# Seven-product SwiGLUs: the w2 product behind two block products, two weight sums by accumulating transfers, token operands formed later

## The chip, the cores and the metric

One core of one Trainium2 chip runs the whole program in one launch. The metric is the device time of that core in microseconds. The kernel before takes 2764.49 us (median of 3 runs, 2763.46 to 2766.02).

## The reference

A two-layer backbone over 512 latent tokens and 256 context tokens of width 1024. Each layer is a half-step SwiGLU, a token mixing, and another half-step SwiGLU; each is preceded by an RMS norm with shift and scale and followed by a gate, and these come from a modulation of a conditioning vector. The change is in the SwiGLUs:

```python
def swiglu(x, w1, w3, w2):
    return (jax.nn.silu(x @ w1) * (x @ w3)) @ w2

def macaron_half(h, m, i, g, w1, w3, w2):
    y = swiglu(modulate(rms_norm(h, g), m[:, 3 * i], m[:, 3 * i + 1]), w1, w3, w2)
    return h + 0.5 * m[:, 3 * i + 2, None, :] * y
```

D_MODEL is 1024 and D_FF 2816. All is float32. The modulation of a layer is `silu(c) @ w_ada[l] + b_ada[l]`, nine vectors of 1024 for the latent and nine for the context tokens.

## The kernel before

Tokens lie in columns (768: first 256 context, then 512 latent), channels on the partitions. To keep float32 accuracy, each operand of a matmul is split into a high and a low part (`hi`, `lo`, both fp32r): ScalarE makes `hi` by a cast, VectorE `lo` by a subtraction (`split_psum`, L403 and L404; with a factor L406 and L407). A product is then three matmuls, hi*hi, hi*lo and lo*hi (`mm3`, L396 to L398).

There are four SwiGLUs. The first runs in a plain form (`ffn`). The other three run in `ffn7`: the second of layer 0 (here A, from about 1003 us), the first of layer 1 (B, from about 1552 us), and the second of layer 1 (C, from about 2420 us, latent tokens alone). `ffn7` goes over the 22 hidden tiles of 128 channels in 11 pairs. The first pair (`first_pair`) is computed plainly. The other ten (`pair(j, ...)`) multiply the 2x2 blocks of weights (2 hidden tiles by 2 halves of the 1024 inputs, w1 and w3 side by side, 128x1024 elements each, blocks r11, r12, r21, r22) by the 2x2 blocks of tokens (2 halves of the inputs by 2 halves of the columns) with seven block products instead of eight, in the manner of Winograd. They are called by their token operand: B11, B21, E, t3, t1, t4, B22. Each is 24 matmuls (2 of w1/w3, 4 of 128 inputs, 3 of hi/lo), of 384 columns in A and B and of 256 in C. B11, B21 and B22 are plain blocks of the normed tokens; E, t4, t3 and t1 are combinations of the kept float32 tokens (`t`, tiles `nf`), formed once for each SwiGLU by `combine` (L835 to L838, sixteen subtractions and additions in all, and the splits) and `combine_rest`. The weights of E, t3, t1 and B22 are sums of blocks, formed in every pair by four VectorE additions (L973, L974, L975, L977). The seven products go to two PSUM areas, Y and X; `snapshot` (ScalarE, L888) copies an area out where a later product is added to it, and `gated` and L993/L994 form silu(w1 part) * (w3 part) into `silu` tiles. `parts` (L869, L870) splits these into `ghi` and `glo`, the token operand of the w2 product.

The w2 product of a pair (`down`, 8 output tiles for the latent and 8 for the context columns; 96 matmuls, in C 48) goes through four PSUM banks B; VectorE adds each result to `h` (L905) and so frees its bank. It is handed to the next pair as `middle()`, and stands there behind the first block product, B11. After each w2 product, `modulate(j)` takes groups of the modulation of layer 1 from a queue: each loads four `ada` tiles (L491) and has VectorE multiply and sum them (`mod_tile`, L483, tile `junk`), with a priority that is 3000 instructions later. `mods` says how many groups each pair takes: one in A's pairs 1 to 8, two in B's.

Weights come through five `raw` buffers (`block`, L798; for w2 `unit`, L388), all by transfers issued by SP, and their split parts through four `w` buffers. Working tiles come from 44 slots that are handed out first in, first out (`m3`, `free`). The order of the instructions on each engine is laid out when the program is built, by a scheduler that takes of the instructions that its model of time has ready the one with the earliest place in the program; each engine then runs its own in that order, and waits where an operand or a buffer isn't there.

Of the kernel before, what the change touches and what calls it, by code (L numbers as in the profile page):

```python
# [12 lines left out]
ALU = mybir.AluOpType  # L13
# [5 lines left out]
T = CTX + SEQ  # L19
# [293 lines left out]
class Builder:  # L313
# [480 lines left out]
    def block(self, src):  # L794

        r = self.mp.tile([128, 1024], F32, tag="raw", name=self.name("raw"), bufs=self.raws)
        if src is not None:
            self.nc.sync.dma_start(r, src)  # L798
        return r

    def split_block(self, r, scale=None):
# [4 lines left out]
    def ffn7(self, l, i, n, t, gate, nxt, streams=(X_COLS, C_COLS), split=None, late=None, mods=()):  # L806
# [14 lines left out]
        halves = X_HALVES if x_only else ((0, T // 2), (T // 2, T))  # L821
        wd = halves[0][1] - halves[0][0]
        n1, n2 = (slice(*c) for c in halves)
        off = {X_COLS: 512, C_COLS: 256}
        np_ = NF // 2
# [2 lines left out]

        tt, box, owned = {}, {}, []

        def combine(k):

            u, v = t[k], t[k + 4]
            tensor = nc.vector.tensor_tensor
            tensor(out=u[:, n1], in0=u[:, n1], in1=u[:, n2], op=ALU.subtract)  # L835
            tensor(out=u[:, n2], in0=v[:, n2], in1=u[:, n2], op=ALU.subtract)
            tensor(out=v[:, n2], in0=u[:, n1], in1=v[:, n2], op=ALU.add)
            tensor(out=v[:, n1], in0=v[:, n2], in1=v[:, n1], op=ALU.subtract)  # L838
            c = slice(halves[0][0], halves[1][1])
            hi, lo = self.hl(T, "c")  # L840
            self.split_psum(hi[:, c], lo[:, c], v[:, c])
            tt[k, "t4"], tt[k, "E"] = ([p[:, q] for p in (hi, lo)] for q in (n1, n2))
            owned.append((hi, lo))
            if k % 2 == 0:
                box["t3"] = self.hl(2 * wd, "c")
                owned.append(box["t3"])
            tt[k, "t3"] = [p[:, k % 2 * wd:k % 2 * wd + wd] for p in box["t3"]]
            self.split_psum(*tt[k, "t3"], u[:, n2])
            self.free(t.pop(k + 4))

        def combine_rest():

            for k in range(4):
                tt[k, "t1"] = [p[:, n2] for p in n[k]]
                self.split_psum(*tt[k, "t1"], t[k][:, n1])
                self.free(t.pop(k))

        def operand(name, k):
            if name in ("B11", "B21", "B22"):
                return [p[:, n1 if name[2] == "1" else n2] for p in n[k + 4 * (name[1] == "2")]]  # L860
            return tt[k, name]


        def gtiles(j):
            for f in (2 * j, 2 * j + 1):
                g[f] = self.hl(T, "g")

        def parts(f, s, cols):
            nc.scalar.copy(g[f][0][:, cols], s[:, cols])  # L869
            nc.vector.tensor_sub(g[f][1][:, cols], s[:, cols], g[f][0][:, cols].bitcast(F32))  # L870

        def product(bank, w, name, start):

            for x in range(2):
                for k in range(4):
                    self.mm3(bank[:, x * 512:x * 512 + wd], [w[:, p, x * 512 + k * 128:x * 512 + k * 128 + 128] for p in range(2)],
                             operand(name, k), start and k == 0, k == 3, not start)
# [7 lines left out]
        def snapshot(bank, base):  # L885
            y = self.m3(2 * wd, base=base)
            v = y.rearrange("p (x c) -> p x c", x=2)
            nc.scalar.copy(v, both(bank))  # L888
            return y, v

        def gated(s, cols, bank, y, sign):

            zv = y[1]
            nc.vector.tensor_tensor(out=zv, in0=both(bank), in1=y[1], op=ALU.add)
            self.last_silu = nc.scalar.activation(s[:, cols], zv[:, 0], AF.Silu, scale=sign)
            nc.vector.scalar_tensor_tensor(out=s[:, cols], in0=zv[:, 1], scalar=sign, in1=s[:, cols], op0=ALU.mult, op1=ALU.mult)
# [59 lines left out]
        def pair(j, middle):  # L956
            fs = (2 * j, 2 * j + 1)
            src = mp13[j]
            add = nc.vector.tensor_add
            Y, X = (self.ps("S", (j + x) % 2) for x in range(2))  # L960
            r11 = self.block(src[0, 0])
            product(Y, self.split_block(r11), "B11", True)
            middle()
            y0 = snapshot(Y, "y")
            gtiles(j)
            s = [self.m3(base="silu") for _ in range(2)]
            r12 = self.block(src[0, 1])
            product(X, self.split_block(r12), "B21", True)
            r21, r22, s1 = self.block(src[1, 0]), self.block(src[1, 1]), self.block(None)
            gated(s[0], n1, X, y0, 1.0)  # L970
            self.free(y0[0])
            parts(fs[0], s[0], n1)
            add(s1, r21, r22)  # L973
            add(r21, r11, r21)  # L974
            add(r11, s1, r11)  # L975
            product(Y, self.split_block(r11, -1.0), "E", False)
            add(r12, r11, r12)  # L977
            y1 = snapshot(Y, "y")
            product(X, self.split_block(r21), "t3", True)
            w0 = snapshot(X, "y")  # L980
            if j == 1:
                combine_rest()
            product(Y, self.split_block(s1), "t1", False)
            gated(s[1], n2, Y, w0, -1.0)
            self.free(w0[0])
            product(X, self.split_block(r22), "t4", False)
            if j == np_ - 1:
                self.free(owned)
            gated(s[1], n1, X, y1, -1.0)
            self.free(y1[0])  # L990
            parts(fs[1], s[1], slice(halves[0][0], halves[1][1]))
            product(Y, self.split_block(r12), "B22", False)
            self.last_silu = nc.scalar.activation(s[0][:, n2], Y[:, 0:wd], AF.Silu)  # L993
            nc.vector.tensor_mul(s[0][:, n2], s[0][:, n2], Y[:, 512:512 + wd])  # L994
            parts(fs[0], s[0], n2)
            self.free(s)

        self.table(AF.Silu, self.norm_sqrt)
        first_pair()
        for k in range(4):  # L1000
            combine(k)

        def middle(j):
            def go():
                ws, fs = second(j), (2 * j, 2 * j + 1)
                for d in range(8):
                    for cols in streams:
                        down(fs, ws, d, cols)
                self.free([g.pop(f) for f in fs])
                modulate(j)  # L1010
            return go
# [737 lines left out]
    def build(self, stop=None):  # L1749
        nc = self.nc  # L1750
        self.setup()
        n = self.new_n()
        begin = Start(self, n)
        for g in range(5, 24):
            self.mod_queue.append(lambda g=g: self.mod_group(0, g, 16))
        for l in range(DEPTH):
            last = l == DEPTH - 1
            ns = 1 if last else 2
            nxt = Next(self, l, 3, SM_GMIX, 2, n)
            if l:  # L1760
                tabs = []
                self.ffn7(l, 0, n, t, self.gate(l, 2, 2, 0.5), nxt, late=lambda: tabs.extend(self.rope_tables(l)), mods=(2,) * 8)
            else:
                self.ffn(l, 0, n, self.gate(l, 2, 2, 0.5), nxt, begin=begin, mods=2)
            assert not self.mod_queue
            if l == 0:
                tabs = self.rope_tables(l)
                self.setup_mixing()
            if stop == (l, 0):
                break  # L1770

            nxt = Next(self, l, 6, SM_GF2, ns, keep=True)
            self.mixing(l, n, tabs, self.gate(l, 5, ns, 1.0), last, nxt)
            n, before = nxt.n, nxt
            if stop == (l, 1):
                break

            if not last:
                self.load_small(l + 1)
                self.silu_c(wide=True)  # L1780
                for g in range(24):
                    self.mod_queue.append(lambda g=g: self.mod_group(1, g))
                nxt = Next(self, l + 1, 0, SM_GF1, 2, n, keep=True)
                self.ffn7(l, 1, n, before.t, self.gate(l, 8, 2, 0.5), nxt, mods=(1,) * 8)
                t = nxt.t
            else:
                self.ffn7(l, 1, n, before.t, self.gate(l, 8, 1, 0.5), Done(self), streams=(X_COLS,), split=X_HALVES)
            if stop == (l, 2):
                break
        if stop is not None:  # L1790
            for k in range(8):
                nc.sync.dma_start(self.a["out"][k], self.h[k])
# [122 lines left out]
```

## Time and profile before

| | |
|---|---|
| median of 3 runs | 2764.49 us (2763.46 to 2766.02) |
| profiled execution's own time | 2769.52 us |
| its span, first to last instruction | 2767.7 us |
| mean granted TensorE clock | 0.984 |
| TensorE matmul busy | 2658.0 us, 96% |
| VectorE busy | 2046.8 us, 74% |
| ScalarE busy | 1087.9 us, 39% |
| GpSimd busy | 278.8 us, 10% |
| read from HBM | 244.90 MB, 89 GB/s over the span |

An engine is busy while one of its instructions runs; overlapping matmuls count once. The granted clock is the share of full TensorE speed (2.4 GHz) that was granted; in this trace a stretch is at 1.0 or at 0.5 (1.2 GHz), and a mean between them says how much of it was at the lower level. "A <- B" in a list of waits says that A's next instruction was ended in its waiting by B. Because the engines run in order, a wait delays all that stands behind it on its engine.

### The profile page before, as it was taken

The page shows a single profiled execution, that of the slowest core. Times are in us where ns is not written, and L with a number is a line of the kernel's source. Part 1 is how long each engine was busy: PE and PEld are TensorE (multiplying, and loading weights), DVE is VectorE, ACT ScalarE, POOL GpSimd, SP SyncE. Part 2 cuts the span into 40 slices and gives each one's busy share as a digit, 9 for nine tenths or more (in the row PEclk, how much of TensorE's full clock was granted, in tenths as well). Part 3 has the DMA queues.
Part 4 walks back from the last instruction along what each step waited for, and adds up shares of the span by engine and source line. Part 5 has one row for each costly group of instructions (what it writes and reads, how often), then busy time and mean ns, then how long its engine had stood idle before and what let it go on. Part 6 is the DMA issues. An engine that isn't in the chain of part 4 may idle for free.

```text
span 2767.7 us, 40029 instructions
## 1 busy us (share of the span) xinstructions
PE 2658.0 (96%) x15788; PEld 2357.8 (85%) x15788; DVE 2046.8 (74%) x3551; ACT 1087.9 (39%) x1895; POOL 278.8 (10%) x370
## 2 busy tenths in 40 slices
PE   7999999999989998999999989999999989999999
PEld 5788888888867788999899879999998877888998
DVE  8986776655775559778676799887756675587886
ACT  4311211124665653233232632323335665544443
POOL 5100000001352210000000100000001352100000
PEclk8899999999989999999999999999999999999999
DMA  7542433211200013233222244443222210123322
GB/s 246 162 136 94 158 117 113 83 54 56 75 22 24 12 46 111 90 102 99 81 75 69 67 125 128 141 144 121 84 76 67 69 32 24 39 80 106 98 93 91
DMA packets 78673, 249.60 MB, mean 90 GB/s; under 512 B 8978, under 2 KB 10642, under 8 KB 78484
## 3 DMA queue, kind: packets, MB, share of 16 engines
q1 hardware_dynamic: 78484, 247.03, 27.6%
q8 instruction: 124, 2.03, 0.3%
q14 instruction: 65, 0.53, 0.1%
HBM read 244.90 MB, written 2.10 MB: 89 GB/s over the span
## 4 chain that ended last, share of the span: by engine, by line
PE 78%; DVE 14%; ACT 3%; issue 3%; DMA 2%; POOL 0%; SPq 0%; DVEq 0%; ACTq 0%; POOLq 0%
PE S L396 14%; PE S L398 13%; PE S L397 13%; PE B L397 10%; PE B L398 10%; PE B L396 10%; PE B L1424 3%; DVE w L404 2%; DVE junk L483 2%; PE B L1575 2%; DVE h L905 1%; DMA raw<-in_w13s 1%; DMA ada<-in_w_ada 1%; ACT w L403 1%; PE B L1543 1%
## 5 line engine op out<-in xcount | busy, mean ns | idle before, releaser
L403 ACT CAST w<-raw 128x1024 fp32r<-128x1024 f32 (+1 forms) x369 | 381.3, 1044 | 723.3 <-issue 330.0
L397 PE MATMUL S<-nlo,w 128*128 128x256 f32 (+2 forms) x1808 | 598.0, 331 | 9.4 <-DVE nlo L605 6.2
L396 PE MATMUL S<-nhi,w 128*128 128x256 f32 (+2 forms) x1808 | 590.0, 332 | 12.7 <-DVE silu L994 4.3
L398 PE MATMUL S<-nhi,w 128*128 128x256 f32 (+2 forms) x1808 | 596.4, 331 | 2.7 <-DVE w L404 2.5
L404 DVE TENSOR_TENSOR w<-raw,w 128x1024 fp32r<-128x1024 f32 (+1 forms) x369 | 449.2, 1229 | 95.3 <-ACT w L403 94.2
L397 PE MATMUL B<-glo,w 128*128 128x512 f32 (+1 forms) x1232 | 425.4, 346 | 5.6 <-DVE glo L870 5.6
L398 PE MATMUL B<-ghi,w 128*128 128x512 f32 (+1 forms) x1232 | 423.0, 346 | 3.1 <-DVE w L404 3.1
L396 PE MATMUL B<-ghi,w 128*128 128x512 f32 (+1 forms) x1232 | 416.2, 348 | 6.4 <-DVE h L905 2.7
L905 DVE SCALAR_TENSOR_TENSOR h<-B,g,h 128x512 f32<-128x512 f32 (+1 forms) x440 | 273.3, 642 | 145.5 <-PE B L398 144.7
L397 PEld LDWEIGHTS S<-nlo,w 128*128 128x128 f32 x1808 | 343.6, 190 | 33.8 <-DVE nlo L605 10.5
L396 PEld LDWEIGHTS S<-nhi,w 128*128 128x128 f32 x1808 | 341.4, 190 | 35.7 <-DVE silu L994 4.3
L398 PEld LDWEIGHTS S<-nhi,w 128*128 128x128 f32 x1808 | 344.2, 190 | 25.8 <-DVE w L404 6.9
L397 PEld LDWEIGHTS B<-glo,w 128*128 128x128 f32 x1232 | 232.0, 188 | 35.5 <-DVE glo L870 6.5
L396 PEld LDWEIGHTS B<-ghi,w 128*128 128x128 f32 x1232 | 229.8, 188 | 37.8 <-DVE h L905 5.1
L483 DVE CUSTOM_DVE_ANT_0 junk<-ada,bc,mpart 128x768 f32<-128x768 f32 x238 | 245.6, 1032 | 20.3 <-DMA ada<-in_w_ada 16.9
L398 PEld LDWEIGHTS B<-ghi,w 128*128 128x128 f32 x1232 | 231.7, 188 | 33.8 <-DVE w L404 3.8
L396 PE MATMUL S<-chi,w 128*128 128x384 f32 (+1 forms) x720 | 232.1, 323 | 13.5 <-ACT y L888 10.7
L398 PE MATMUL S<-chi,w 128*128 128x384 f32 (+1 forms) x720 | 229.1, 321 | 2.7 <-DVE w L404 2.1
L397 PE MATMUL S<-clo,w 128*128 128x384 f32 (+1 forms) x720 | 230.5, 321 | 0.0
L691 DVE SCALAR_TENSOR_TENSOR h<-B,g,h 128x256 f32<-128x256 f32 (+1 forms) x176 | 103.8, 615 | 101.6 <-PE B L398 101.6
L532 POOL TENSOR_TENSOR sq<-sq,sq 128x512 f32<-128x512 f32 (+1 forms) x38 | 42.2, 1112 | 1159.3 <-ACT sq L528 1158.1
L888 ACT COPY y<-S 128x768 f32<-128x768 f32 (+1 forms) x90 | 65.5, 728 | 237.7 <-PE S L398 130.9
(267 smaller groups left out, 4413.6 us busy)
## 6 DMA issues: line engine op xcount, KB each, us to landing
raw<-in_w SPq DMA_DIRECT2D x132, 512.0 KB, 3.6
raw<-in_w13s SPq DMA_DIRECT2D x132, 512.0 KB, 3.8
ada<-in_w_ada SPq DMA_DIRECT2D x171, 384.0 KB, 4.0
raw<-in_w_out SPq DMA_DIRECT2D x16, 512.0 KB, 4.3
ada<-in_ada SPq DMA_DIRECT2D x16, 384.0 KB, 6.4
raw<-in_w_in_t SPq DMA_DIRECT2D x10, 512.0 KB, 3.5
raw<-in_dftx SPq DMA_DIRECT2D x8, 512.0 KB, 3.5
ada<-in_ada SPq DMA_DIRECT2D x8, 256.0 KB, 5.2
```

What stands on the lines that cost most here:

```text
L396: mm(out, lhs[0], rhs[0], start=start, stop=False, skip_group_check=more)
L397: mm(out, lhs[0], rhs[1], start=False, stop=False, skip_group_check=more)
L398: mm(out, lhs[1], rhs[0], start=False, stop=stop, skip_group_check=more)
L403: nc.scalar.copy(hi, src)
L404: nc.vector.tensor_sub(lo, src, hi.bitcast(F32))
L483: nc.vector.tensor_tensor_reduce(out=self.junk[:, 0:w.shape[1]], in0=w, in1=v, scale=1.0, scalar=init, op0=ALU.mult, op1=ALU.add, accum_ou ...
L532: (nc.vector if part else nc.gpsimd).tensor_add(st[key], st[key], t)
L691: nc.vector.scalar_tensor_tensor(out=self.h[d][:, c0:c1], in0=ps[:, 0:c1 - c0], scalar=gate()[:, d, s:s + 1], in1=self.h[d][:, c0:c1], op0 ...
L888: nc.scalar.copy(v, both(bank))
L905: nc.vector.scalar_tensor_tensor(out=self.h[d][:, c0:c1], in0=ps[:, 0:c1 - c0], scalar=gate()[:, d, s:s + 1], in1=self.h[d][:, c0:c1], op0 ...
L1424: mm(outs[y], lhs[y], rhs[y], start=start, stop=stop)
L1575: nc.tensor.transpose(pt[:, x * 256 + i * 128:x * 256 + i * 128 + 128], Ps[i, y][:, tok(kp * 2 + x)], self.ident)
```

## The change

- In `pair`, the weights of B11 and B21 are loaded first; both products stand ahead of `middle()`, so a pair's w2 product stands behind two block products of the next pair. New `g` tiles are taken after it.
- Two of the four sums leave VectorE. `block_sum` loads the first block with SP and adds the second by a transfer that GpSimd issues with `accum_op=ALU.add`: s1 = r21 + r22 and s3 = r11 + r21 (the former r21). r22 is loaded by itself; r11 and r21 are read twice. A pair has seven loads of w1/w3 blocks instead of four.
- `combine` is called by operand within pair 1: "E" behind the w2 product, "t4" and "t3" (with t1) behind E; before, all but t1 was formed between `first_pair` and pair 1. The sum for B22 stands behind t1.
- The groups of modulation move from pairs 1 to 8 to pairs 3 to 10 (`mods`), in A and B.

```diff
+    def block_sum(self, *srcs):
+        r = self.block(srcs[0])
+        for src in srcs[1:]:
+            self.nc.gpsimd.dma_start(out=r, in_=src, accum_op=ALU.add)
         return r
...
-        def combine(k):
...
+        def combine(name):
             for k in range(4):
+                u, v = t[k], t[k + 4]
+                if name == "E":
+                    tensor(out=u[:, n1], in0=u[:, n1], in1=u[:, n2], op=ALU.subtract)
+                    tensor(out=u[:, n2], in0=v[:, n2], in1=u[:, n2], op=ALU.subtract)
+                    tensor(out=v[:, n2], in0=u[:, n1], in1=v[:, n2], op=ALU.add)
+                    tensor(out=v[:, n1], in0=v[:, n2], in1=v[:, n1], op=ALU.subtract)
+                    box[k] = self.hl(T, "c")
+                    owned.append(box[k])
+                    parts_of("E", k, [p[:, n2] for p in box[k]], v[:, n2])
+                elif name == "t4":
+                    parts_of("t4", k, [p[:, n1] for p in box[k]], v[:, n1])
+                    self.free(v)
+                else:
+                    parts_of("t1", k, [p[:, n2] for p in n[k]], u[:, n1])
...
+                    parts_of("t3", k, [p[:, k % 2 * wd:k % 2 * wd + wd] for p in box["t3"]], u[:, n2])
+                    self.free(u)
...
-            r11 = self.block(src[0, 0])
+            first = combine if j == 1 else lambda name: None
+            r11, r12 = self.block(src[0, 0]), self.block(src[0, 1])
             product(Y, self.split_block(r11), "B11", True)
-            middle()
             y0 = snapshot(Y, "y")
-            gtiles(j)
+            product(X, self.split_block(r12), "B21", True)
             s = [self.m3(base="silu") for _ in range(2)]
-            r12 = self.block(src[0, 1])
-            product(X, self.split_block(r12), "B21", True)
-            r21, r22, s1 = self.block(src[1, 0]), self.block(src[1, 1]), self.block(None)
             gated(s[0], n1, X, y0, 1.0)
             self.free(y0[0])
+            middle()
+            gtiles(j)
             parts(fs[0], s[0], n1)
-            add(s1, r21, r22)
-            add(r21, r11, r21)
+            s1, s3, r22 = self.block_sum(src[1, 0], src[1, 1]), self.block_sum(src[0, 0], src[1, 0]), self.block(src[1, 1])
+            first("E")
             add(r11, s1, r11)
             product(Y, self.split_block(r11, -1.0), "E", False)
-            add(r12, r11, r12)
             y1 = snapshot(Y, "y")
-            product(X, self.split_block(r21), "t3", True)
+            first("t4")
+            first("t3")
+            product(X, self.split_block(s3), "t3", True)
             w0 = snapshot(X, "y")
-            if j == 1:
-                combine_rest()
             product(Y, self.split_block(s1), "t1", False)
             gated(s[1], n2, Y, w0, -1.0)
             self.free(w0[0])
+            add(r12, r11, r12)
             product(X, self.split_block(r22), "t4", False)
...
-        for k in range(4):
-            combine(k)
...
-                self.ffn7(l, 0, n, t, self.gate(l, 2, 2, 0.5), nxt, late=lambda: tabs.extend(self.rope_tables(l)), mods=(2,) * 8)
+                self.ffn7(l, 0, n, t, self.gate(l, 2, 2, 0.5), nxt, late=lambda: tabs.extend(self.rope_tables(l)), mods=(0,) * 2 + (2,) * 8)
...
-                self.ffn7(l, 1, n, before.t, self.gate(l, 8, 2, 0.5), nxt, mods=(1,) * 8)
+                self.ffn7(l, 1, n, before.t, self.gate(l, 8, 2, 0.5), nxt, mods=(0,) * 2 + (1,) * 8)
```

## Rows read from the trace of the kernel before

**Rows 1.** Page, part 1: busy us, share of the span, instructions.
```profile
PE 2658.0 (96%) x15788; PEld 2357.8 (85%) x15788; DVE 2046.8 (74%) x3551; ACT 1087.9 (39%) x1895; POOL 278.8 (10%) x370
```
**Rows 2.** Stretches: length, each engine's busy us, granted clock, DMA share, GB/s.
```profile
1035.00:1104.00 69.00, 62.04 (x350) 57.13 (x348) 67.56 (x124) 28.59 (x42) 0.00 (x0) 0.98 0.36 111
1104.00:1401.00 297.00, 284.54 (x1569) 269.01 (x1569) 231.31 (x382) 88.63 (x113) 0.00 (x0) 0.98 0.30 94
1401.00:1500.00 99.00, 99.00 (x563) 94.55 (x563) 68.25 (x85) 32.04 (x41) 0.00 (x0) 1.00 0.21 68
1590.00:1686.00 96.00, 82.21 (x454) 75.54 (x452) 93.35 (x180) 27.53 (x38) 0.00 (x0) 0.95 0.38 118
1686.00:1968.00 282.00, 280.26 (x1587) 264.50 (x1586) 239.06 (x405) 89.94 (x116) 0.00 (x0) 1.00 0.43 134
2420.00:2470.00 50.00, 45.87 (x329) 42.40 (x329) 47.51 (x77) 28.62 (x51) 0.00 (x0) 1.00 0.22 74
2470.00:2722.00 252.00, 249.30 (x1719) 229.48 (x1718) 201.45 (x247) 105.06 (x151) 0.00 (x0) 1.00 0.31 101
```
**Rows 3.** Tile ada in A: duration ns min/median/max, first and last start us.
```profile
L483 DVE CUSTOM_DVE_ANT_0 junk<-ada,bc,mpart x48: 1005/1016/1028, 1056.5 to 1398.6; 128x768 f32<-128x768 f32 x48
```
**Rows 4.** TensorE's waits, 1104 to 1401: us in total, times, longest.
```profile
PE B L397 <- DVE glo L870: 4.9, 3, 2.4
PE S L396 <- DVE silu L994: 2.6, 3, 0.9
PE S L398 <- DVE w L404: 2.1, 3, 0.9
PE S L396 <- ACT w L406: 2.0, 1, 2.0
```
**Rows 5.** Timeline of VectorE at a pair's end in A: start, us, instruction.
```profile
1149.78 1.22 DVE L973 TENSOR_TENSOR raw<-raw,raw 128x1024 f32<-128x1024 f32 x1
...
1152.45 1.22 DVE L974 TENSOR_TENSOR raw<-raw,raw 128x1024 f32<-128x1024 f32 x1
...
1154.53 0.95 DVE L870 TENSOR_TENSOR glo<-silu,ghi 128x768 fp32r<-128x768 f32 x1
```
**Rows 6.** TensorE's waits, 1590 to 1686.
```profile
PE S L396 <- ACT y L888: 7.8, 2, 5.3
```
**Rows 7.** ScalarE's waits, 1590 to 1686.
```profile
ACT y L888 <- DVE mpart L483: 2.8, 1, 2.8
```
**Rows 8.** VectorE's groups by form, 1590 to 1686: busy us, mean ns, idle before.
```profile
L483 DVE CUSTOM_DVE_ANT_0 junk<-ada,bc,mpart 128x768 f32<-128x768 f32 x23 | 23.3, 1013 | 0.2
...
L483 DVE CUSTOM_DVE_ANT_0 junk<-ada,bc,sml 128x256 f32<-128x256 f32 x23 | 11.0, 480 | 0.3
...
L838 DVE TENSOR_TENSOR nf<-nf 128x384 f32<-128x384 f32 x4 | 2.2, 546 | 0.0
```
**Rows 9.** Timeline of TensorE in a w2 product of B.
```profile
1724.74 0.39 PE L398 MATMUL B<-ghi,w 128*128 128x512 f32 x1
1724.97 0.28 PE L396 MATMUL B<-ghi,w 128*128 128x256 f32 x1
...
1726.04 0.28 PE L396 MATMUL B<-ghi,w 128*128 128x256 f32 x1
```
**Rows 10.** Line 798's loads of 512 KB, whole span: issue to landing.
```profile
DMA to landing us min/median/max: 3.3/3.8/6.6
```
**Rows 11.** SP's queue, waits, 2470 to 2691.
```profile
SPq L798 <- DVE w L407: 86.7, 7, 13.8
```
**Rows 12.** Line 798's loads, 2470 to 2722: who waited (us, times), issue to landing.
```profile
  DVE raw L973: 4.5, 6
...
DMA to landing us min/median/max: 3.3/4.4/5.6
```
**Rows 13.** Page, part 5: a group of ScalarE.
```profile
L403 ACT CAST w<-raw 128x1024 fp32r<-128x1024 f32 (+1 forms) x369 | 381.3, 1044 | 723.3 <-issue 330.0
```

More of the change, by code (lines that the diff above doesn't have):

```diff
@@ L796, in block @@
         r = self.mp.tile([128, 1024], F32, tag="raw", name=self.name("raw"), bufs=self.raws)
-        if src is not None:
-            self.nc.sync.dma_start(r, src)
+        self.nc.sync.dma_start(r, src)
+        return r
+    def block_sum(self, *srcs):
+        r = self.block(srcs[0])
+        for src in srcs[1:]:
+            self.nc.gpsimd.dma_start(out=r, in_=src, accum_op=ALU.add)
         return r
@@ L829, in ffn7, with parts_of @@
         tt, box, owned = {}, {}, []
-        def combine(k):
-            u, v = t[k], t[k + 4]
+        def parts_of(name, k, parts, src):
+            tt[k, name] = parts
+            self.split_psum(*parts, src)
+        def combine(name):
             tensor = nc.vector.tensor_tensor
[L835 to L849, printed above, removed]
@@ L851, in combine_rest @@
-        def combine_rest():
-            for k in range(4):
-                tt[k, "t1"] = [p[:, n2] for p in n[k]]
-                self.split_psum(*tt[k, "t1"], t[k][:, n1])
-                self.free(t.pop(k))
+            for k in range(4):
+                u, v = t[k], t[k + 4]
[12 more added lines that the diff above has]
+                    parts_of("t1", k, [p[:, n2] for p in n[k]], u[:, n1])
+                    if k % 2 == 0:
+                        box["t3"] = self.hl(2 * wd, "c")
+                        owned.append(box["t3"])
+                    parts_of("t3", k, [p[:, k % 2 * wd:k % 2 * wd + wd] for p in box["t3"]], u[:, n2])
+                    self.free(u)
@@ L985, in pair @@
             self.free(w0[0])
+            add(r12, r11, r12)
             product(X, self.split_block(r22), "t4", False)
-            if j == np_ - 1:
-                self.free(owned)
             gated(s[1], n1, X, y1, -1.0)
@@ L992, in pair @@
             product(Y, self.split_block(r12), "B22", False)
+            if j == np_ - 1:
+                self.free(owned)
             self.last_silu = nc.scalar.activation(s[0][:, n2], Y[:, 0:wd], AF.Silu)
```

## The prediction, made before the change was run

> **What bounds the kernel now.** I read the page's busy shares first: TensorE is busy 96% of the span, VectorE 74% [rows 1]. So only time in which TensorE waits, or runs at its lower clock, can be won. The change touches three seven-product SwiGLUs, which I call A (from 1003 us), B (from 1552) and C (from 2420; latent tokens only). Next I read the table of stretches. What a stretch loses is its length less the time TensorE is busy, plus its length times (1 - granted clock), since a part at half clock counts as busy [rows 2]:
> - A, up to the first pair's end (1035 to 1104): 69 - 62.0 + 1.4 = 8.3 us.
> - A, six pairs (1104 to 1401): 297 - 284.5 + 5.9 = 18.4, so 3.1 a pair. The two pairs after them, 1401 to 1500, lose nothing; A's last modulation sum starts at 1398.6 [rows 3].
> - B, first pair (1590 to 1686): 96 - 82.2 + 4.8 = 18.6. Six pairs (1686 to 1968): 1.7.
> - C, first pair (2420 to 2470): 4.1. Eight pairs (2470 to 2722): 2.7.
>
> Together 53.8 us: all that the change could win, 1.9% of the time.
>
> Then I asked what ended TensorE's waits. In A's six pairs [rows 4] it waits for `glo` (the w2 product's operand) three times, up to 2.4 us; for the silu product of line 994 three times, and for the splits of the E and t3 blocks (L406, L404) four times. The VectorE timeline at a pair's end says why [rows 5]: sums for the next pair's blocks (L973, L974, 1.22 us each) stand ahead of the `glo` that TensorE wants. In B's first pair TensorE waits 7.8 us for the snapshot y [rows 6], and that waited on ScalarE for VectorE's modulation sums [rows 7], whose tiles it reuses. In that stretch VectorE is busy 93.35 of 96 us [rows 2], 23 x (1.01 + 0.48) = 34 us of it modulation [rows 8].
>
> **The change part by part.** TensorE's own work stays: seven products and one w2 product a pair. Matmuls follow each other in 0.119 us at 256 columns (nine steps from 1724.97 to 1726.04) and 0.23 at 512 [rows 9]. So in C a product (24 matmuls) takes 2.9 us, the w2 product 48 x 0.23 = 11.0, a pair 31.0. In A and B the w2 product takes 48 x (0.23 + 0.119) = 16.8; B's six pairs take 47.0 each, 0.3 of it lost [rows 2], so a product there takes (46.7 - 16.8) / 7 = 4.3.
>
> *w2 behind B21.* Now `glo` has only B11 as cover after the last product; then it has B11 and B21, 4.3 us more in A and B, 2.9 in C. The longest `glo` wait was 2.4 us: those go. B21 writes the bank that line 994 reads, so what is late next is that silu product, with B11 alone as cover, as now. The E and t3 blocks, whose splits TensorE waited for (2.0 + 2.1 us), now have the whole w2 product between B21 and them in program order: these go. I keep 0.43 a pair for the silu (0.86 us in every other pair), and some 0.4 for what clock and small waits remain: 0.8. The modulation groups stand in eight pairs as before, now the third to the tenth. A's pairs: 18.4 - 8 x 0.8 = 12.0 us won. In B two more pairs get modulation at 0.3 each: 0.6 lost. In C the splits of w2 (the small waits there) have 2.9 us more cover: 2.7 to 1.5, 1.2 won.
>
> *Two of four sums go to transfers.* VectorE loses 2 x 1.22 us a pair [rows 5], 73 us over 30 pairs. None of it counts in the sum by itself: VectorE was not the last in the pairs without waits. It adds 3 loads of 512 KB a pair, two of them accumulating, issued by POOL, which has no other work in these pairs. No row shows an accumulating transfer. From below: as a plain load of the same size, 3.3 us at the least; below that is excluded, since it moves the same bytes and reads the destination too. From above: two of the longest plain landings, 13.2 us [rows 10]. I take twice the median, 7.6.
>
> What hides it: there are five raw buffers for seven blocks a pair, and SP waits for them as it is [rows 11]. The base of s1 gets the buffer that the last block of the pair before (r12, for B22) leaves when it is split, at the latest a product before the pair's end. In C from there to E: 3 x 2.9 + 11.0 = 19.7 us, less the load (4.4, [rows 12]), the sum that stays (1.2), and the split on ScalarE (1.0, [rows 13]) and VectorE (1.2): 11.9 us for the accumulation. In A and B: 3 x 4.3 + 16.8 - 3.8 - 3.4 = 22.5. At 7.6 it is hidden in all three; at 13.2, C would wait 1.3 us in each of 10 pairs, 13 us. r11 and r12 are held longer (the sum for B22 moves behind t1), but both of the next pair are loaded when s3 and r11 leave theirs, during the w2 product, well ahead.
>
> The Trainium skill, "Collectives: The Full Stack", section on the bandwidth ceiling, says that a reducing transfer runs at about half the rate of a copy, because the add needs two source reads (1.93 measured there). By it the accumulation would be an estimated 7 to 9 us here, and the sum as it is; no run before shows it.
>
> *Operands later, modulation later.* Forming the operands is 16 combinations and 16 splits of 384 columns at 0.55 us [rows 8], the same work as before, but the twelve splits for t4, t1 and t3 stand behind E. Modulation leaves the first two pairs. In B's first stretch VectorE drops from 93 us by 34 (modulation) and 5 (sums of two pairs); even with all 32 x 0.55 = 17.6 us of forming pushed into it, it has about 72 us of work for the 77 (96 - 18.6) that TensorE needs. So VectorE no longer sets the end, and the y snapshot no longer waits for modulation. What is late next is t3: 12 x 0.55 + 1.22 = 7.8 us of VectorE against E's 4.3 us, up to 3.5 late if none of it is done in the w2 product, nothing if all is; I take 2. The last of E's operands gets a slot that the w2 product leaves, so it comes after it: 1 us. With 1 to 2 us of waits for the norm's `nlo`, which stay, I leave 4 us in A, 5 in B, and in C, with 256 columns and no modulation, 2.5. Won: 4.3 + 13.6 + 1.6.
>
> Sum: 12.0 - 0.6 + 1.2 + 4.3 + 13.6 + 1.6 = 32.1 us. The profiled execution took 2769.5 us (span 2767.7 and 1.8 around it), so it becomes 2737.4. The median shown, 2764.5, lies 5.0 below the profiled execution; with the same difference the forecast is 2732.4 us.
>
> **The rivals.**
> 1. *A's waits move with the modulation.* B has twice the modulation a pair and hardly a wait, which speaks against it; that A's two free pairs lose nothing speaks for it. If all eight pairs keep 3.1 us, A's term is 18.4 - 24.8 = -6.4 instead of 12.0, and the time 2750.8.
> 2. *It does not do what it says.* The order on every engine is the scheduler's, which lays work where its model sees room: it may still lay sums ahead of `glo` and form the operands as early as before. A's pairs then keep 3.1, and the first pairs win half: -6.4 - 0.6 + 0.6 + 2.2 + 6.8 + 0.8 = 3.4, so 2761.1.
> 3. *Slower: the sum that stays blocks VectorE.* Line 975's sum waits for the accumulated s1, and VectorE works in order: behind it stand the h updates that free the four banks of the w2 product. If s1 lands later than the order was laid out for, TensorE goes on for four banks: 4 x 16.8 / 16 = 4.2 us in A and B, 4 x 11.0 / 8 = 5.5 in C. Beyond, each us counts in 30 pairs. Slower by 0.2% from 20 (d - 4.2) + 10 (d - 5.5) = 37.6, d = 5.9 us. With the order laid out for a plain load (3.8), twice the median is d = 3.8, no loss; 13.2 is d = 9.4. At d = 7: 56 + 15 = 71 us, 2803. For it: VectorE already waits for loads before the first sum of C's pairs, 4.5 us in six waits [rows 12]. Against it: the buffers' slack above. The Trainium skill, "SBUF — State Buffer", the "DVE blocks DMA" trap, says that transfers issued by GpSimd starve while VectorE runs a mode with two ports, such as copies; VectorE's forms here are sums and splits with two inputs, so by that page it should not bite, and no run before shows it.
>
> **How the numbers follow.** Forecast 0.60 (own range 2718 to 2747), rival 1 0.17, rival 2 0.08, rival 3 0.12, and 0.03 that nearly all 53.8 us go, 2711. The range 2712 to 2762 takes in the first three and leaves out rival 3. About 0.2%, 5.5 us, is what a measurement can tell from no change: 2759 to 2770. Rival 2 lies at its edge, so 0.07 for the same, 0.81 faster, 0.12 slower.
>
> **What would show it.** Right: no `glo` waits of TensorE in A's pairs; its waits in B's first stretch down to about 5 us; six pairs in A at about 282 us, as in B; 60 fewer sums on VectorE; accumulating transfers landing in 5 to 10 us, and no wait of VectorE's sum for them. Wrong: VectorE idle before line 975's sum with a transfer as its end (rival 3), A's pairs still at 49 us (rival 1), or TensorE waiting for t3 or t1 operands for much more than 2 us in the first pairs.

## The result and the profile after

The changed kernel took 2832.4 us (median of 4 runs, 2831.3 to 2832.7), the kernel before 2765.3 beside it: 1.0243 of its time, 95% interval 1.0225 to 1.0261. It is 67 us slower; 32 us faster had been forecast. The profiled execution took 2832.1 us (span 2830.3).

Page of the kernel after, part 1 (busy us, share of the span, instructions) [rows 1]:
```profile
PE 2669.8 (94%) x15788; PEld 2368.4 (84%) x15788; DVE 1981.9 (70%) x3503; ACT 1089.0 (38%) x1907; POOL 336.0 (12%) x430
```
VectorE is rid of 65 us of work, as meant. TensorE has the same 15788 matmuls, idles 51 us more and is busy 12 us longer, at a mean granted clock of 0.979 against 0.984. Since the matmuls are the same in both kernels, a stage can be compared from its first matmul to its last, by number. Us more (+) or less (-) than before, from one profiled execution of each; the columns are named by the times of before. In the first 1000 us, ahead of A, where no edit reaches, the profiled executions of this document differ from that of before by -2.0 to +4.0 us, so 2 or 3 us in one column are no finding by themselves:

| kernel | A 1st pair (1035) | A six pairs (1104) | two more (1401) | A's end, to B (1500) | B 1st (1590) | B six (1686) | B's end, mixing (1968) | between (2097) | C 1st (2420) | C rest (2470) |
|---|---|---|---|---|---|---|---|---|---|---|
| after | -3.4 | +26.1 | +16.4 | +6.8 | -13.5 | +8.4 | +4.7 | +2.8 | +2.5 | +12.6 |

The first pairs of A and B won about what was forecast. The pairs behind them lost more than that, A's by far the most. Stretches of the kernel after that answer to the A, B and C rows of [rows 2] (same columns):
```profile
1102.00:1423.00 321.00, 287.46 (x1570) 270.88 (x1569) 211.08 (x346) 88.94 (x113) 10.43 (x12) 0.96 0.40 117
...
1635.00:1718.00 83.00, 79.40 (x455) 73.70 (x454) 59.32 (x89) 32.02 (x50) 2.63 (x3) 1.00 0.32 90
1718.00:2008.00 290.00, 281.45 (x1586) 265.35 (x1586) 235.14 (x426) 89.10 (x113) 10.46 (x12) 1.00 0.54 162
```
A's six pairs lose 321 - 287.5 + 0.04 x 321 = 46 us where they lost 18.4. VectorE is less busy there than before, 211 of 321 us, so it is not short of time. TensorE's waits in that stretch (us, times, longest; compare [rows 4]):
```profile
PE S L396 <- DVE y L902: 23.3, 5, 5.0
PE S L396 <- ACT y L896: 7.4, 5, 1.5
PE B L396 <- DVE h L913: 1.4, 1, 1.4
```
The `glo` waits are gone, as forecast; a wait for `y` of line 902 (the sum in `gated`) has come, 4.7 us in the mean in five of six pairs. VectorE at such a place, its timeline (start, us, instruction, idle before it and what ended that):
```profile
1346.66 1.23 DVE L404 TENSOR_TENSOR w<-raw,w 128x1024 fp32r<-128x1024 f32 x1 [0.63 <-ACT w L403]
1356.09 1.23 DVE L982 TENSOR_TENSOR raw<-raw,raw 128x1024 f32<-128x1024 f32 x1 [8.21 <-DMA raw<-in_w13s]
1357.23 1.82 DVE L902 TENSOR_TENSOR y<-S,y 128x768 f32<-128x768 f32 x2
...
1361.23 1.02 DVE L904 SCALAR_TENSOR_TENSOR silu<-y,silu 128x384 f32<-128x384 f32 x2
```
and TensorE there:
```profile
1358.24 0.45 PE L396 MATMUL S<-nhi,w 128*128 128x384 f32 x1 [4.52 <-DVE y L902]
```
ScalarE's silu of line 1000, which reads B22's result, follows 24 matmuls later:
```profile
1364.29 0.49 ACT L1000 ACTIVATE silu<-S 128x384 f32<-128x384 f32 x1 [1.17 <-PE S L398]
```
and the chain of waits there (start us, us, what) has s1's base load and the accumulating transfer one behind the other:
```profile
1344.90 1.14 DVE w L404
1346.06 3.85 DMA raw<-in_w13s
...
1350.58 5.42 DMA raw<-in_w13s
1356.09 0.50 DVE raw L982
```
Line 982 is `add(r11, s1, r11)` of the *next* pair, waiting for the accumulated s1. Queued behind it are both `gated` sums of the pair that is ending. The first reads the bank Y, to which B22, the last product of that same pair, is added; the second reads X, which the next pair's B11 overwrites. The product that begins at 1358.24 is B22, so TensorE stops in the ending pair already. Line 982 over the whole kernel (idle of VectorE before it, times):
```profile
  DMA raw<-in_w13s: 123.2, 27
```
27 of 30 sums wait, 4.6 us each. In C it is the silu product of line 1001 that stands behind; it reads B22's bank, which the next pair's B21 overwrites (TensorE's waits, 2520 to 2783):
```profile
PE S L396 <- DVE silu L1001: 12.8, 7, 2.9
```
The transfers (issue to landing, us) of the accumulating line:
```profile
DMA to landing us min/median/max: 5.3/5.8/8.5
```

### The profile page after: what moved, and what is told of

Its sections match the earlier page's. It is cut to its first block, busy times and chain, and to the rows that moved or that the text cites. A ratio compares the mean times of both kernels' runs of the same rounds, so it can differ in the third digit from the quotient of the medians.

```text
span 2830.3 us, 40236 instructions
## 1 busy us (share of the span) xinstructions
PE 2669.8 (94%) x15788; PEld 2368.4 (84%) x15788; DVE 1981.9 (70%) x3503; ACT 1089.0 (38%) x1907; POOL 336.0 (12%) x430
## 3 DMA queue, kind: packets, MB, share of 16 engines
q1 hardware_dynamic: 82804, 262.76, 27.1%
## 4 chain that ended last, share of the span: by engine, by line
PE 40%; DMA 10%; DVE 9%; issue 2%; ACT 2%; POOL 1%; POOLq 0%; DVEq 0%; ACTq 0%; SPq 0%
DMA raw<-in_w13s 9%; PE S L396 7%; PE S L397 6%; PE S L398 6%; PE B L396 6%; PE B L397 6%; PE B L398 6%; DVE w L404 2%; PE B L1429 1%; DVE junk L483 1%; DVE h L913 1%; DMA ada<-in_w_ada 1%; PE B L1580 1%; ACT w L403 1%; DVE raw L982 1%
## 5 line engine op out<-in xcount | busy, mean ns | idle before, releaser
L396 PEld LDWEIGHTS S<-nhi,w 128*128 128x128 f32 x1808 | 345.3, 192 | 84.3 <-DVE y L902 37.1
L397 PEld LDWEIGHTS S<-nlo,w 128*128 128x128 f32 x1808 | 347.9, 192 | 36.0 <-DVE nlo L605 12.9
L398 PEld LDWEIGHTS S<-nhi,w 128*128 128x128 f32 x1808 | 348.5, 193 | 18.2
L398 PEld LDWEIGHTS B<-ghi,w 128*128 128x128 f32 x1232 | 232.3, 189 | 32.1 <-DVE w L404 0.3
L804 POOL DMA_DIRECT2D raw<-in_w13s x60 | 52.4, 874 | 1298.4 <-DMA raw<-in_w13s 397.2
L396 PEld LDWEIGHTS S<-chi,w 128*128 128x128 f32 x720 | 135.3, 188 | 16.3 <-ACT y L896 12.9
```

Source lines behind the costliest of these rows:

```text
L396: mm(out, lhs[0], rhs[0], start=start, stop=False, skip_group_check=more)
L397: mm(out, lhs[0], rhs[1], start=False, stop=False, skip_group_check=more)
L398: mm(out, lhs[1], rhs[0], start=False, stop=stop, skip_group_check=more)
L804: self.nc.gpsimd.dma_start(out=r, in_=src, accum_op=ALU.add)
```

## The experiments

Each run had the kernel before beside it on the same chip. The quoted text is what was expected. The numbers behind it are the median, then the ratio to the kernel before with its 95% interval. All stage tables of this section in one place (us against before, same columns as above):

| kernel | A 1st | A six | two more | A's end | B 1st | B six | B's end | between | C 1st | C rest |
|---|---|---|---|---|---|---|---|---|---|---|
| e1, sums on VectorE | -5.7 | -6.4 | +5.6 | +5.1 | -17.0 | +11.2 | +5.4 | +3.6 | -0.9 | -5.2 |
| e2, sum held | -3.4 | -6.1 | +5.1 | +7.3 | -12.9 | -0.5 | +8.5 | +2.6 | +1.3 | +28.7 |
| e3, s1 loaded first | -3.0 | -6.1 | +5.7 | +6.1 | -13.3 | +17.5 | +8.1 | +3.1 | +5.8 | +27.6 |
| e4, transfers alone | -2.0 | -8.3 | +1.6 | -0.4 | +0.8 | +9.2 | +0.4 | +1.0 | +4.7 | +48.3 |
| e5, old modulation | -2.2 | -3.5 | +2.6 | +4.0 | -5.2 | +8.5 | +0.1 | +2.3 | -0.9 | -5.2 |
| e6, s3 only | -5.3 | -13.4 | +1.7 | +6.6 | -14.3 | +12.7 | +9.9 | +3.9 | -0.8 | -5.2 |
| e7, w2 alone | +7.2 | -3.6 | +2.3 | +0.2 | +7.5 | +2.4 | -0.1 | +2.1 | +2.2 | -5.1 |
| e8, a block fewer | -3.7 | +27.1 | +15.7 | +6.9 | -12.0 | +8.9 | +3.1 | +3.3 | +3.0 | +11.2 |
| e9, by stage | -4.9 | -13.2 | +1.7 | +0.7 | -13.4 | +4.6 | 0.0 | +2.2 | -0.9 | -5.8 |
| e10, two free | -4.8 | -13.2 | +1.7 | +6.2 | -14.0 | +2.6 | +7.5 | +4.6 | -0.9 | -5.1 |
| e11, plain second | -6.2 | +8.8 | +12.9 | +9.5 | -14.4 | -2.1 | +3.1 | +1.9 | +0.1 | -3.0 |
| e12, s1 only | -6.3 | -6.1 | +5.0 | +8.3 | -17.2 | +0.1 | +6.3 | +0.5 | -2.5 | -5.1 |

**e1.** (`block(None)` takes a buffer and loads nothing.)
```diff
-            s1, s3, r22 = self.block_sum(src[1, 0], src[1, 1]), self.block_sum(src[0, 0], src[1, 0]), self.block(src[1, 1])
+            r21, r22, s1 = self.block(src[1, 0]), self.block(src[1, 1]), self.block(None)
+            add(s1, r21, r22)
+            add(r21, r11, r21)
+            s3 = r21
```


> The kernel after, with both weight sums back on VectorE (s1 and r21 by tensor_add, r21 loaded by SP as in the kernel before); order of products, late operands and modulation stay as in the kernel after. Theory T (VectorE's remaining sum waits for the accumulated s1 and holds up the work of the previous pair that is queued behind it): without accumulating transfers that wait goes; A's pairs 2 to 7 lose at most what they lost before (about 297 us for six), the first pairs keep their gain (A -3, B -13), so 2735 to 2765 us. Rival R (w2 behind B21 by itself makes weight loads late, since a raw buffer comes free later): the loss stays, 2800 us or more, with the sums still idle on transfers for over 80 us.

2764.1 us, 0.9987 (0.9977 to 0.9997), line 986's sum never idle on a transfer. T held, R fell: the transfers, with what waits for them, cost 68 us, 2.5%, and all the rest of the change together wins about 0.1%.

**e2.**
```diff
-            add(r11, s1, r11)
+            if "mul" in held:
+                with self.tc.issue_after(held["mul"].ins):
+                    add(r11, s1, r11)
+            else:
+                add(r11, s1, r11)
...
-            nc.vector.tensor_mul(s[0][:, n2], s[0][:, n2], Y[:, 512:512 + wd])
+            held["mul"] = nc.vector.tensor_mul(s[0][:, n2], s[0][:, n2], Y[:, 512:512 + wd])
```


> The kernel after, with one edit: the sum add(r11, s1, r11) may be put on VectorE only behind the last product of the previous pair's silu (tensor_mul of s[0], n2). The two accumulating transfers stay. Theory T: the transfers keep their 5.8 us and their late base load, but nothing that TensorE wants next stands behind the waiting sum; the E product has the w2 product as cover: 2740 to 2775 us, and TensorE's waits for y and silu fall from about 36 us to under 15. Rival Q (the accumulated block itself comes too late for the E product): TensorE then waits for E's split instead, 2805 us or more.

2796.3 us, 1.0106 (1.0085 to 1.0127): neither range. By stage it divides: A's six pairs are as without transfers (-6.1, in e1 -6.4) and B's are better (-0.5, in e1 +11.2), so there T holds, the place of one instruction on VectorE was the whole loss. C lost 29 us. The chain of waits in one pair of C there (start us, us, what):
```profile
2572.15 5.41 DMA raw<-in_w13s
...
2580.48 6.73 DMA raw<-in_w13s
2587.31 1.06 ACT w L403
2588.39 1.23 DVE w L404
2589.62 0.67 DVE h L913
2590.33 0.50 PE B L396
```
The second transfer is s3's. Its split waits on ScalarE, the split's low part on VectorE behind it, and the h update that frees a bank of the w2 product behind that. So in C it is again an in-order queue, held by the next instruction that needs an accumulated block: Q's mechanism, at the t3 operand and not at E. Waits of TensorE in C's pairs (the `glo` of the second stands behind the held sum):
```profile
PE B L396 <- DVE h L913: 16.2, 8, 3.0
PE B L397 <- DVE glo L878: 4.7, 6, 1.6
```

**e3.**
```diff
+            s1 = self.block_sum(src[1, 0], src[1, 1])
             middle()
...
-            s1, s3, r22 = self.block_sum(src[1, 0], src[1, 1]), self.block_sum(src[0, 0], src[1, 0]), self.block(src[1, 1])
+            s3, r22 = self.block_sum(src[0, 0], src[1, 0]), self.block(src[1, 1])
```


> The kernel after, with one edit: s1's base load and accumulating transfer are issued ahead of the w2 loads of the same pair (ahead of middle()). Theory T with its cause in the start of the base load: s1 lands 3 to 8 us earlier, the sum's idle time falls from 123 us to under 60, the time to 2770 to 2805 us. Rival (the raw buffer, not the w2 loads ahead in SP's queue, sets the start): the load starts when the buffer comes free as before, the sum's idle time stays over 100 us, 2820 us or more.

2821.7 us, 1.0198 (1.0182 to 1.0213). The idle time before the sum fell as T said, yet the time stayed as its rival said:
```profile
  DMA raw<-in_w13s: 45.0, 12
```
A recovered; B and C did not. In C's pairs TensorE still waits for line 902 behind the sum (28.4 of the 45 us are there):
```profile
PE S L396 <- DVE y L902: 20.3, 8, 2.9
```
Loading s1 earlier helps only where it gets early enough. B's six pairs are 9 us longer than in the kernel after. There the waits show the pattern of e2's C: ScalarE waits 45.8 us for transfers ahead of its splits (18.0 in the kernel after), and TensorE for h updates (3.7 there). No run tests that this is the cause. ScalarE's and TensorE's waits in B's six pairs:
```profile
ACT w L403 <- DMA raw<-in_w13s: 45.8, 6, 9.5
```
```profile
PE B L396 <- DVE h L913: 9.4, 5, 2.5
```

**e4.** The kernel before with `block_sum` and
```diff
-            r21, r22, s1 = self.block(src[1, 0]), self.block(src[1, 1]), self.block(None)
+            s1, r21, r22 = self.block_sum(src[1, 0], src[1, 1]), self.block_sum(src[0, 0], src[1, 0]), self.block(src[1, 1])
...
-            add(s1, r21, r22)
-            add(r21, r11, r21)
```


> The kernel before, with the two accumulating transfers alone (w2 product, operands and modulation as before). Theory T: the sum waits here too, as the base load waits for the same raw buffer: 10 to 60 us slower than before, 2775 to 2825 us, with VectorE idle on transfers before the sum for over 60 us. Rival S (only with the w2 product behind B21 does the sum get into the way): within 6 us of before, 2758 to 2770 us, and little idle time before the sum.

2825.9 us, 1.0209 (1.0188 to 1.0229); the sum idles 108.2 us in 27 cases. That is 1 us over T's range, and T's mechanism is there without the w2 product's move. But the price follows what stands behind: in A the sum waits 24.1 us and the pairs are 8.3 us *shorter* than before, in C it waits 39.7 us and the pairs grow from 252 to 294 us. VectorE's and TensorE's waits in C's pairs:
```profile
DVE raw L980 <- DMA raw<-in_w13s: 39.7, 7, 6.1
```
```profile
PE S L396 <- DVE silu L999: 27.1, 7, 4.3
```
The waits are not the whole price: the mean granted clock of the stretch is 0.91, where [rows 2] had 1.00, and TensorE's busy time rose from 249.3 to 266.9 us:
```profile
2475.00:2769.00 294.00, 266.87 (x1718) 246.71 (x1718) 181.54 (x225) 104.34 (x148) 13.74 (x16) 0.91 0.47 125
```

**e5.** e1 with
```diff
-mods=(0,) * 2 + (2,) * 8
+mods=(2,) * 8
...
-mods=(0,) * 2 + (1,) * 8
+mods=(1,) * 8
```


> Both weight sums on VectorE as in e1, w2 behind B21 and late operands as in the kernel after, but the modulation groups in the first to eighth pairs as in the kernel before. Theory M (the two pairs' delay of the modulation gives back what it wins): against e1 the two pairs past A's six win 5 us, A's end 4, B's six pairs 8 or more and B's end with the mixing 6; B's first pair gives back up to 17 and A's up to 6: 2738 to 2758 us. Rival (the place of the modulation doesn't matter, since VectorE has room in every pair): 2760 to 2770 us.

2771.7 us, 1.0020 (1.0011 to 1.0030). Theory M fell as a sum: the late stages win back 3.0, 1.1, 2.7, 5.3 and 1.3 us, but the first pairs give back 3.5 and 11.8 and A's six pairs 2.9. The rival's range is missed by 2 us, and its reason fell too: the delay is worth some 8 us net, and most of what B's first pair won is the modulation's leaving.

**e6.** e1 with
```diff
-            r21, r22, s1 = self.block(src[1, 0]), self.block(src[1, 1]), self.block(None)
-            add(s1, r21, r22)
-            add(r21, r11, r21)
-            s3 = r21
+            s1, r22, s3 = self.block(src[1, 0]), self.block(src[1, 1]), self.block_sum(src[0, 0], src[1, 0])
+            add(s1, s1, r22)
```


> As e1, but s3 = r11 + r21 comes by an accumulating transfer (s1 = r21 + r22 by VectorE in place): one accumulating transfer a pair, and no instruction of VectorE adds its result; only the split reads it. Theory T (a sum on VectorE that waits for a transfer is what costs): at most as long as e1, 2745 to 2768 us, C no longer than in e1. Rival U (accumulating transfers cost by themselves: the buffer is held through two loads in a row, so that all loads come later): 2780 us or more, C longer by 15 us or more.

2762.9 us, 0.9982 (0.9972 to 0.9993). T held: here an accumulating transfer that no sum of VectorE waits for costs nothing, in C neither. In A's six pairs it wins 7 us on e1.

**e7.** The kernel before with `middle()` and `gtiles(j)` moved behind B21 and its `gated`, and r12 loaded beside r11.


> The kernel before with one edit: the w2 product stands behind B11 and B21 (r12 loaded beside r11); sums, operands and modulation as before. Prediction's step: A's six pairs win about 12 us, C 1, so 2750 to 2758 us, and no glo waits. Rival (the w2 product's place is worth nothing, the waits move to another operand of the same stretch): 2762 to 2772 us.

2789.3 us, 1.0085 (1.0065 to 1.0105): slower, which neither side had. The steady pairs win a little (A -3.6, C -5.1), the first pairs of A and B lose 7 each. TensorE's waits there, A's first pair and then B's, and what ScalarE's snapshot waited for in B's:
```profile
PE S L396 <- ACT y L888: 10.5, 1, 10.5
...
PE S L396 <- ACT y L888: 19.0, 1, 19.0
```
```profile
ACT y L888 <- DVE mT L483: 10.4, 2, 9.6
```
This is the wait of [rows 6, 7], grown: with operands and modulation both in the first pair, the w2 product's move makes it worse. The later operands (e5 against e7, 18 us) are not enough to make the move pay; with the later modulation too it comes out 0.1% ahead (e1).

**e8.**
```diff
-            s1, s3, r22 = self.block_sum(src[1, 0], src[1, 1]), self.block_sum(src[0, 0], src[1, 0]), self.block(src[1, 1])
+            s1, s3 = self.block_sum(src[1, 0], src[1, 1]), self.block_sum(src[0, 0], src[1, 0])
...
-            product(X, self.split_block(r22), "t4", False)
+            product(X, self.split_block(s1), "t4", False)
```


> The kernel after, with the block r22 left out (t4's product takes a second split of s1; the result is another one): six loads into five buffers a pair in place of seven, all matmuls, splits and sums kept. Theory T with the buffers as the cause of the late base load: the base of s1 starts a block earlier, the sum's idle time falls from 123 to under 50 us, and the time to 2750 to 2790 us. Rival V (the accumulating transfer's own length, or SP's place behind the w2 loads, is the cause): idle time over 90 us, 2810 us or more.

2834.0 us, 1.0247 (1.0229 to 1.0264): nothing moved, as V said (line 982's idle):
```profile
  DMA raw<-in_w13s: 121.6, 27
```
A block fewer changes nothing, so the number of raw blocks is not the cause. The chain of waits says what times the base load:
```profile
1345.71 1.14 DVE w L404
1346.87 4.09 DMA raw<-in_w13s
1351.02 0.60 issue
1351.62 5.43 DMA raw<-in_w13s
```
It starts with the end of a split. That and the two transfers in series were left as causes.

**e11.**
```diff
-            self.nc.gpsimd.dma_start(out=r, in_=src, accum_op=ALU.add)
+            self.nc.gpsimd.dma_start(out=r, in_=src)
```


> The kernel after, with the second transfer into s1 and s3 as a plain one that overwrites (the sum is left out, the result is another one); order, buffers and issue stay. Theory W (it is the second transfer standing behind the first that makes s1 late, not the adding): the second lands in 4 to 5 us instead of 5.8, the sum's idle time falls from 123 to 85 to 115 us, and the time to 2800 to 2826 us. Rival (the adding has a price of its own, several us): idle time under 50, the time below 2790 us.

2781.0 us, 1.0058 (1.0043 to 1.0073): the time is in the rival's range, the idle time between the two. Landing of the second transfer, and line 982's idle:
```profile
DMA to landing us min/median/max: 3.6/4.0/7.2
```
```profile
  DMA raw<-in_w13s: 76.9, 27
```
The adding makes one transfer 1.8 us longer (5.8 against 4.0). The sum waits 1.7 us less in each of 27 pairs (46 in all), and the kernel is 51 us shorter, at a mean granted clock of 0.983 against 0.979. s3's transfer is shorter here too, and its part was not separated. The rest of the wait, 77 us, stays with the second transfer standing behind the first; no run takes that alone away.

**e12.**
```diff
-            s1, s3, r22 = self.block_sum(src[1, 0], src[1, 1]), self.block_sum(src[0, 0], src[1, 0]), self.block(src[1, 1])
+            s1, r21, r22 = self.block_sum(src[1, 0], src[1, 1]), self.block(src[1, 0]), self.block(src[1, 1])
+            add(r21, r11, r21)
+            s3 = r21
```


> The kernel after, with s1 alone by transfer; s3 = r11 + r21 is made by VectorE, r21 loaded by SP. Theory T (the sum that waits for s1 is the whole loss): 2815 to 2840 us, idle time before the sum over 100 us. Rival (two accumulating transfers a pair, one behind the other on POOL, are what makes s1 late): 2765 to 2795 us.

2750.5 us, 0.9950 (0.9935 to 0.9965). T's number fell, by 65 us, and the rival's was 15 too high. s1 still comes by an accumulating transfer (5.3/5.5/7.3 us), and the sum that adds it, now line 984, is never idle. VectorE's timeline shows why:
```profile
1328.80 1.82 DVE L902 TENSOR_TENSOR y<-S,y 128x768 f32<-128x768 f32 x2 [5.51 <-PE S L398]
...
1336.84 1.23 DVE L981 TENSOR_TENSOR raw<-raw,raw 128x1024 f32<-128x1024 f32 x1 [0.68 <-DMA raw<-in_w13s]
...
1340.52 1.22 DVE L984 TENSOR_TENSOR raw<-raw,raw 128x1024 f32<-128x1024 f32 x1
```
r11 is an operand of line 981 too, so the sum has to follow it, and line 981 waits for a block that is loaded later. That puts both behind the `gated` of the pair that ends: the order that e2 wrote by hand. So "a sum waits for s1" was too wide a statement; what counts is how early it is queued. e12 takes s3's transfer away as well, so it is e2 that shows this for A and B. In C either transfer alone costs nothing ("C rest" -5.1 here, -5.2 in e6); with both, C loses (+28.7 in e2).

**e9 and e10**, from these: A with s3 by transfer, B with both and the sum held, C with neither. The edit of e9, without the lines that hold the sum (as in e2); e10 keeps `(0,) * 2`:
```diff
+            if acc == "both":
+                s1, s3, r22 = self.block_sum(src[1, 0], src[1, 1]), self.block_sum(src[0, 0], src[1, 0]), self.block(src[1, 1])
+            elif acc == "s3":
+                s1, r22, s3 = self.block(src[1, 0]), self.block(src[1, 1]), self.block_sum(src[0, 0], src[1, 0])
+                add(s1, s1, r22)
+            else:
+                r21, r22, s1 = self.block(src[1, 0]), self.block(src[1, 1]), self.block(None)
...
-mods=(0,) * 2 + (2,) * 8
+mods=(0,) + (2,) * 8, acc="both"
...
-mods=(0,) * 2 + (1,) * 8
+mods=(0,) + (1,) * 8, acc="s3"
```


> The kernel after with each of its stages at the setting that was best there: A with s3 alone by transfer (e6), B with both by transfer and the sum held behind the previous pair's silu product (e2), C with both sums on VectorE (e1); modulation leaves only the first pair, not two. If the stages are independent: A's first pair -5, its six pairs -13, B's first pair -13, its six pairs 0, C -6, and the modulation that spills past the pairs' end in A and B (11 and 6 us in e2 and e6) at most half of that: 2736 to 2752 us. Rival (the gains of one stage are taken back at the next one, as B's six pairs did in e1 and e6): 2756 to 2766 us.

> As e9, with modulation out of the first two pairs as in the kernel after. Theory M2 (modulation that starts at the third pair spills past the last pairs): 3 to 8 us longer than e9, all of it past the sixth modulated pair in A and B. Rival: within 2 us of e9, or shorter, since B's second pair has no modulation.

e9: 2740.4 us, 0.9914 (0.9899 to 0.9929), faster than both kernels. The stages add, but for B's six pairs (+4.6, where 0 was expected). e10: 2752.6 us, 0.9948 (0.9931 to 0.9964). The second free pair costs 12 us more, somewhat over what was expected, nearly all at A's and B's ends (5.5 and 7.5), where modulation stands in the way after the pairs. Page of e9, part 1:
```profile
PE 2646.8 (97%) x15788; PEld 2352.2 (86%) x15788; DVE 2012.3 (73%) x3533; ACT 1088.3 (40%) x1907; POOL 306.1 (11%) x400
```
and the waits of TensorE that are left in A's six pairs:
```profile
PE S L396 <- ACT y L897: 4.7, 6, 0.8
```

## Why the prediction was wrong

**The step that failed** is the cover of the remaining sum, "What hides it" and rival 3 alike. The text measured the transfer against E, the next product that *needs* the block, and for a late block it put the h updates behind the sum, with four banks of cover. In the trace the two `gated` sums of the pair before (in C the silu product) stand behind it, and the next TensorE product (in A the ending pair's own B22, in C the next pair's B21) needs their bank at once. In the pair shown s1 had landed by 1356.1, some 20 us before E's first matmul, and yet TensorE lost 4.5 us. Over the kernel the sum idled 123 us, which the forecast had at nothing. The rival had the mechanism; its break-even of 5.9 us and its 0.12 rest on the wrong neighbour. Its 2803 at d = 7 was still 29 us short. Shown by e2: moved behind that silu product, the same sum of the same late block costs nothing in A and B. There the cover worked out against E was enough. In C (11.9 us by the text) TensorE never waits for E's block in e2 either: it waits 16.2 us behind the split of s3, which the text did not cost at all, and 4.7 us for the `glo` behind the held sum.

**The transfer's size** was not the mistake: 5.3 to 8.5 us, median 5.8, where 7.6 was taken. The Trainium skill, "Collectives: The Full Stack", section on the bandwidth ceiling, would have a reducing transfer at half the rate of a copy; here it took 5.8 against 4.0 us in the same place (e11), 1.45 times, so the measurement decides for less. The Trainium skill's figure is a rate of collectives between ranks, this one a time to landing.

**The buffers** as the slack that sets the start of s1's base load: the text counted seven loads a pair into five buffers, but the two w2 loads (L388) go through the same five, so there are nine. A block fewer left the start where it was (e8). It follows a split; what paces that split was not tried. In the pair shown it starts at 1346.06, more than a product before the pair's end, as the text had it.

**w2 behind B21.** A's six pairs were to win 12.0 and won 6.4 without the transfers (e1); the move alone won 3.6 (e7). The `glo` waits went; others came (e1, A's six pairs):
```profile
PE B L396 <- DVE h L914: 5.8, 5, 1.3
PE S L396 <- ACT y L897: 4.8, 5, 1.0
```
With s3 by transfer they won 13 (e6, e9). In C it won 5, four times the 1.2 forecast. That the move alone makes the first pairs 7 us longer had not been seen.

**The first pairs** were right in kind: A -3.4 and B -13.5 in the kernel after, where -4.3 and -13.6 were forecast. That B agrees to 0.1 us is luck: without the transfers it won 17.0 and A 5.7 (e1). 11.8 of B's 17.0 are the modulation's leaving (e5). TensorE's waits in B's first pair, against 7.8 us [rows 6]:
```profile
PE S L397 <- DVE nlo L605: 1.7, 1, 1.7
```
C's first pair lost 2.5 instead of winning 1.6, through the transfers (e1: -0.9).

**The modulation's new place** was costed at 0.6 us. By e5 against e1 the stretches past A's six pairs and past B's lose 10.7 us by it and B's six pairs 2.7; e9, with one free pair, is 12 us shorter than e10. A's last modulation sum, which began at 1398.6 [rows 3], begins past A's end in the kernel after:
```profile
L483 DVE CUSTOM_DVE_ANT_0 junk<-ada,bc,mpart x48: 1005/1013/1355, 1145.6 to 1596.5; 128x768 f32<-128x768 f32 x48
```
B's six pairs lose 8.5 to 12.7 us where VectorE makes s1 and the operands are late (e1, e5, e6), and less where s1 comes by transfer without blocking (nothing in e2 and e12, 4.6 and 2.6 in e9 and e10). So in B the sums seem to count, against "none of it counts in the sum by itself". But e7, with all sums on VectorE, loses only 2.4 there; the cause was not isolated and stays open.

Without the transfers, then, 32.1 us forecast are 4.3 in e1's profile: first pairs +23.6, A's and C's pairs +11.6, B's six pairs -11.2, the ends and the two pairs past A's six -19.7. With the transfers that is -63.4 in the kernel after: they cost 68.

## What to carry to other kernels

When an engine's work goes to a transfer, look up what is queued behind the first instruction that now waits for it, not only when its result is needed: holding back one sum won 36 of the 67 us lost, though C lost 15 more by it (e2). Hold such an instruction behind the work that frees the next bank, or give it an operand that arrives late. Choose stage by stage: the two transfers with the sum held cost nothing in the long pairs of A and B and 29 us in the short ones of C. Work moved out of a busy pair must be counted where it lands, at the far end of the row too.

## What had not been expected of the hardware

A second transfer on GpSimd's queue occupies that engine for 866 ns when it accumulates and 528 when it overwrites. Line 804 in the kernel after, and then in e11 (ns min/median/max):
```profile
L804 POOL DMA_DIRECT2D raw<-in_w13s x60: 853/866/1023, 1011.6 to 2785.5; - x60
```
```profile
L804 POOL DMA_DIRECT2D raw<-in_w13s x60: 527/528/743, 1010.9 to 2733.3; - x60
```
A wait of VectorE for a transfer need not cost: in e4 24 us of it in A went with pairs that were 8 us shorter, while in C 40 us of it lengthened the kernel by 48. Some 18 of those 48 are TensorE's longer busy time at the lower mean clock.
